# Activations as the stationary operand, four weight tiles per product: the second part of a one-core encoder block

## The chip, the cores and the metric

The kernel runs on one core of a Trainium2 chip. The metric is the time of one execution on the device, in microseconds (us). A separate profiled execution gives the trace and the page of the profile.

## What is computed

One encoder layer on 256 tokens of 2048 features, all in fp32:

```python
u = rmsnorm(h, g1);  z = u @ w_in          # [B_a C_a V_a | q k v | gate_a gate_b]
y_a = (b_a * dwconv3(c_a * v_a)) @ w_out_a
y_b = windowed_attention(rope(q), rope(k), v, sink) @ w_o_attn
h = h + (sigmoid(gl_a + ba) * y_a + sigmoid(gl_b + bb) * y_b) @ w_mix_out
up = dwconv3(rmsnorm(h, g2) @ ffn_w_up) + bias;  a, g = split(up)   # 2 x 5632
h = h + (silu(a) * g) @ ffn_w_down
return rmsnorm(h, g3)
```

Nearly all the work is in the matrix products. There are 243 MB of fp32 weights (60.8 million), each of which is used once, with 256 tokens.

## The kernel before

Features lie on the partitions (128 at a time, a *tile*), the 256 tokens in the free dimension. A job computes one tile of 128 output features: for each of its k blocks of 128 input features it takes one block of 128x128 weights and the activations of that block (128 features x 256 tokens). To keep fp32 accuracy in the fp32r format, both are split into a high and a low part, and three of the four cross products are summed: high weights with high activations, high weights with low activations, low weights with high activations. High and low activations lie side by side, so the first two are one product of 512 columns (line 215), and the third is one of 256 columns (line 216). The weights are the stationary operand and the activations move. One bank of PSUM holds both halves of the sum; `total` (L243) copies one half to SBUF on ScalarE (L245) and adds the other to it on VectorE (L249). A *pair* below is the two products of one k block of one tile.

`run` (L131) cuts all jobs into chunks of eight weight blocks (512 KB) and writes out the order of every engine by hand. For each chunk c it issues the fetch of chunk c+6 on SyncE's DMA queue (`fetch`, L155, five buffers), the high part of chunk c+3 on ScalarE (`high`, L165), the low part of chunk c+2 on VectorE (`low`, L180, three buffers), and then the products of chunk c. After each chunk one step of every open epilogue is issued; an epilogue is a generator, and `yield 1` means "go on after the next chunk". So the engines' queues hold fetches, splits and epilogues in a fixed order, and an instruction that waits holds up those issued after it on its engine. `turns` swaps the two products of a few pairs (`turned` in `run`), so that there a 256-column product follows a 256-column one, and a 512-column one a 512-column one.

The stages, in the order of the work: a first part (q, k, v, conv branch, attention); the gates (32 tiles of `w_in`, 16 k blocks each); `w_oa` and `w_o` in turn (16 tiles each, 8 k blocks); `w_mix` (16 tiles, 16 k blocks); `w_up` (88 tiles, 16 k blocks); `w_dn` (16 tiles, 44 k blocks). At the start of `w_mix`, `w_up` and `w_dn` a few jobs are interleaved by k (`outer_first`, L629), so that their first products don't wait for the last results of the stage before. The last tile of `w_dn` is computed in halves of the tokens, to shorten the tail (`finale`, L687). After the attention and after the second norm, `turns` is asked for.

The epilogues: `scaled` (L367) multiplies by the norm's factor; `epi_gate`, `epi_ya`, `epi_yb`, `epi_mix`, `epi_up` and `epi_dn` (L587 to L685) do the rest. `sumsq` (L288) sums squares for the next norm on GpSimd, two instructions for each tile.

Of the kernel before, what the change touches and what calls it, by code (L numbers as in the profile page):

```python
# [26 lines left out]
CH = 8  # L27
WIDE = 6
# [23 lines left out]
def hybrid_block_kernel(ctx: ExitStack, tc: tile.TileContext, head, wide, xT, w_in, w_oa, w_o, w_mix, w_up, w_dn, vec, cst, out):  # L52
# [4 lines left out]
    spool = ctx.enter_context(tc.tile_pool(name="spool", bufs=2))  # L57
    lin = ctx.enter_context(tc.tile_pool(name="lin", bufs=3, space=PSUM))
# [4 lines left out]
    ct = cpool.tile([P, C_END], F32, tag="ct", name="ct")  # L63
# [3 lines left out]
    ident = ct[:, C_ID : C_ID + P]  # L67
# [62 lines left out]

    def run(groups):  # L131

# [5 lines left out]
        for size, jobs, wide in groups:  # L138
            n = jobs[0][1]
            if wide:  # L140
                for k in range(n):
                    chunks.append((None, [(job, k) for job in jobs], wide))
                continue
            for k0 in range(0, n, size):
                k1 = min(n, k0 + size)
                for job in jobs:
                    chunks.append((job[0][:, k0:k1, :], [(job, k) for k in range(k0, k1)], None))
        raws, his, los, banks = {}, {}, {}, {}

        def pieces(c):  # L150

            n = len(chunks[c][1])
            return ((0, 2), (2, n)) if c < 3 else ((0, n),)

        def fetch(c):  # L155
            w, blocks, pre = chunks[c]
            if pre is not None:
                raws[c] = pre(0, c)
            else:
                raw = wpool.tile([P, CH, P], F32, tag="raw", name="raw", bufs=5)  # L160
                nc.sync.dma_start(raw[:, : len(blocks), :], w)
                raws[c] = lambda a, b, raw=raw: raw[:, a:b, :]


        def high(c):  # L165
            _, blocks, pre = chunks[c]
            if pre is not None:
                pre(1, c)
            (_, _, _, _, *halves), k0 = blocks[0]
            if halves:  # L170
                last = lazy("last", lambda: cpool.tile([P, FT, P], F32R, tag="B", name="last"))
                his[c] = last[:, k0 : k0 + len(blocks), :]
            else:
                his[c] = wpool.tile([P, CH, P], F32R, tag="whi", name="whi")
            for a, b in pieces(c):
                nc.scalar.copy(his[c][:, a:b, :], raws[c](a, b))  # L176
            if pre is not None:
                pre(2, c)
# [11 lines left out]
        for c, (_, blocks, _) in enumerate(chunks):  # L190
# [7 lines left out]
            for i, (job, k) in enumerate(blocks):  # L198
                _, n, rhs, epi, *halves = job
# [5 lines left out]
                a, last, half = rhs(k), k == n - 1, bool(halves and k)  # L205
                if order["due"] and n == KT:
# [7 lines left out]
                products = [  # L214
                    lambda: nc.tensor.matmul(both, hi[:, i, :], moving, start=k == 0, stop=last and turned),  # L215
                    lambda: nc.tensor.matmul(  # L216
                        ps[:, 0:T], lo[:, i, :], a[:, 0:T], start=False, stop=last and not turned
                    ),
                ]
# [23 lines left out]
    def total(ps, dst=None):  # L243
        b = spool.tile([P, T], F32, tag="evb", name="evb")
        nc.scalar.copy(b, ps[:, T : 2 * T])  # L245
        yield 1
        if dst is None:
            dst = spool.tile([P, T], F32, tag="evt", name="evt")
        nc.vector.tensor_tensor(dst, ps[:, 0:T], b, op=ALU.add)  # L249
        return dst  # L250

    rr = {}

    def inv_rms(parts, r, tag="tp"):
# [6 lines left out]
        r0 = spool.tile([P, T], F32, tag="sq", name="r0")[:, 0:n]  # L261
        nc.scalar.activation(r0, acc, AF.Ln, bias=eps)
        v = spool.tile([P, T], F32, tag="evt", name="nv")[:, 0:n]
# [4 lines left out]
        t = spool.tile([P, T], F32, tag="evs", name="nt")[:, 0:n]  # L268
# [19 lines left out]
    def sumsq(k, src, acc):  # L288
        sq = spool.tile([P, T], F32, tag="sq", name="sq") if k else acc
# [5 lines left out]
    p1 = p0.enter_context(tc.tile_pool(name="p1", bufs=1))  # L295


    HEAD = KT + 4 * P
    hd = p1.tile([P, HEAD], F32, tag="hd", name="hd")
    hb = p1.tile([P, WIDE, P], F32, tag="hb", name="hb")  # L300

# [53 lines left out]
    def r1():  # L355
# [5 lines left out]
        yield from inv_rms([sq1[:, 0, :]], new_r("r1"))  # L361
# [5 lines left out]
    def scaled(ps, dst=None):  # L367
        t = yield from total(ps)
        if dst is None:
            dst = spool.tile([P, T], F32, tag="evs", name="evs")  # L370
        nc.vector.tensor_tensor(dst, t, rr["r"], op=ALU.mult)
        return dst
# [228 lines left out]
    def epi_yb(m, ps):  # L601
        gates = box["gates"]
        t = yield from total(ps)
        nc.vector.tensor_tensor(t, t, gates[:, KT + m, :], op=ALU.mult)
# [6 lines left out]
    def epi_mix(m, ps):  # L611
        yield 1
        for i in range(2):
            nc.vector.tensor_tensor(x[:, m, :], x[:, m, :], ps[:, i * T : i * T + T], op=ALU.add)
# [8 lines left out]
    for i in range(2 * KT):  # L623
        groups.append(single(w_in[len(rest) + i], KT, xr, lambda ps, i=i: epi_gate(i, ps)))
    for m in range(KT):
        groups.append(single(w_oa[m], 8, lambda k: box["B"][:, k, :], lambda ps, m=m: epi_ya(m, ps)))
        groups.append(single(w_o[m], 8, lambda k: box["B"][:, 8 + k, :], lambda ps, m=m: epi_yb(m, ps)))

    def outer_first(jobs, n):  # L629

        groups.append((4, jobs[:n], None))
        groups.extend((CH, [job], None) for job in jobs[n:])

    outer_first([(w_mix[m], KT, lambda k: merged()[:, k, :], lambda ps, m=m: epi_mix(m, ps)) for m in range(KT)], 3)


    def start_ffn():
# [4 lines left out]
        return actA, actC  # L642
# [7 lines left out]
    def r2():  # L650
        nc.scalar.preload_act_table_set("natural_log_exp_and_others")
        yield from inv_rms([acc2], new_r("r2"))
        later(10, turns)

    def epi_up(i, which, ps):
        c = i + which * FT
        t = yield from scaled(ps)
        yield 1
        lazy("act", start_ffn)
# [10 lines left out]
        else:  # L670
            s = half.pop(i)
# [4 lines left out]
    def epi_dn(m, ps):  # L676
        yield 1
# [4 lines left out]
        for i in range(2):  # L682
            nc.vector.tensor_tensor(h, h, ps[:, i * T : i * T + T], op=ALU.add)
# [3 lines left out]
    def finale(ps):  # L687
# [24 lines left out]
        def norm(half):  # L712

            h = x[:, m, cols(half)]
            sq = spool.tile([P, T], F32, tag="sq", name="sq")[:, 0:H]
            nc.scalar.square(sq, h)
            nc.tensor.matmul(sums[half], ones, sq, start=False, stop=True)  # L717
            ln = spool.tile([P, T], F32, tag="evb", name="ln")[:, 0:H]
            nc.scalar.activation(ln, sums[half], AF.Ln, bias=eps)  # L719
            v = spool.tile([P, T], F32, tag="evt", name="nv")[:, 0:H]  # L720
            nc.vector.tensor_scalar(v, sums[half], EPS, None, op0=ALU.add)
            r0 = spool.tile([P, T], F32, tag="sq", name="r0")[:, 0:H]
            nc.scalar.activation(r0, ln, AF.Exp, scale=-0.5)
            nc.scalar.mul(h, h, col(V_GFIN + m))
            t = spool.tile([P, T], F32, tag="evs", name="nt")[:, 0:H]
# [40 lines left out]
    jobs = []  # L766
    for i in range(FT):
        for which in range(2):
            epi = lambda ps, i=i, which=which: epi_up(i, which, ps)
            jobs.append((w_up[2 * i + which], KT, lambda k: hsplit()[:, k, :], epi))  # L770
    outer_first(jobs, 3)
    jobs = [(w_dn[m], FT, act, lambda ps, m=m: epi_dn(m, ps)) for m in range(KT - 1)]
    outer_first(jobs + [(w_dn[KT - 1], FT, act, finale, True)], 2)
# [23 lines left out]
def _layout(a):  # L797
# [5 lines left out]

    def cols(v):
# [15 lines left out]
    order += range(g0, g0 + 2 * D)  # L820
    up = []
    for i in range(FT):
# [22 lines left out]
        "w_oa": tiles(a["w_out_a"][0]),  # L845
        "w_o": tiles(a["w_o_attn"][0][att, :]),
        "w_mix": tiles(a["w_mix_out"][0]),
        "w_up": tiles(a["ffn_w_up"][0][:, up]),
        "w_dn": tiles(a["ffn_w_down"][0]),
# [23 lines left out]
```

## Time and profile before

| | |
|---|---|
| time, 3 runs | 1331.04 us median (1330.96 to 1332.08) |
| profiled execution | 1332.0 us, of which the span of its instructions is 1330.2 us |
| TensorE (PE) busy | 1320.0 us, 99% of the span |
| VectorE (DVE) busy | 955.7 us, 72% |
| ScalarE (ACT) busy | 723.1 us, 54% |
| GpSimd (POOL) busy | 70.1 us, 5% |
| DMA | 255.54 MB, mean 192 GB/s, queue q1 59.1% of 16 engines |
| first and last start of a 512-column product: gates and all before | 6.3 to 409.1 us |
| `w_oa` and `w_o` | 409.4 to 497.8 us |
| `w_mix` | 498.2 to 586.6 us |
| `w_up` | 586.9 to 1075.2 us |
| `w_dn` | 1075.6 to 1304.0 us, then the last tile |

How to read it: a matmul's recorded duration runs from its start to the modelled end of its drain, so neighbours overlap and durations must not be added; the step from one start to the next is what a product costs. PE is matmuls and PEld weight loads, which run beside them. A group of instructions names the line, the engine, the operation, the tiles (out<-in), the shapes, the count, then busy time and mean duration. A wait of an engine is named by who ended it.

### The profile page before, as it was taken

The numbers are of one execution on the slowest core, as the hardware profiler recorded it, in microseconds if no ns is written. First come the engines' busy times: TensorE is split into PE (matmuls) and PEld (weight loads), VectorE is DVE, ScalarE is ACT, GpSimd is POOL, SyncE is SP. The second block draws the span as 40 slices with busy tenths as digits, with TensorE's granted clock in tenths as the row PEclk, the third lists the DMA queues.
The fourth block names the chain that finished last, engine by engine and source line by source line (L and its number), as shares of the span: only waits on it lengthen the run. The fifth ranks groups of instructions, "written<-read, shape, count | busy, mean of one in ns | idle before, by whom it ended". The sixth has DMA issues, their size and how long they took to land.

```text
span 1330.2 us, 20480 instructions
## 1 busy us (share of the span) xinstructions
PE 1320.0 (99%) x7686; PEld 1161.4 (87%) x7686; DVE 955.7 (72%) x1508; ACT 723.1 (54%) x1151; POOL 70.1 (5%) x66
## 2 busy tenths in 40 slices
PE   9999999999999999999999999999999999999997
PEld 8888888888888888888888888888888888888886
DVE  7888777555557887668888888888888865445444
ACT  7667665555555545446555555555555545444442
POOL 0000000000000002430000000000000001111211
PEclk9999999999999999999999999999999999999999
DMA  8786545555555547547555555555555557666663
GB/s 309 234 243 200 199 158 175 182 191 190 191 189 190 190 143 236 188 141 235 190 190 190 191 190 190 190 191 190 191 190 190 174 153 236 194 186 183 197 191 104
DMA packets 76676, 255.54 MB, mean 192 GB/s; under 512 B 8864, under 2 KB 9248, under 8 KB 76576
## 3 DMA queue, kind: packets, MB, share of 16 engines
q1 hardware_dynamic: 76144, 253.44, 59.1%
q8 instruction: 60, 0.98, 0.3%
q10 hardware_dynamic: 432, 0.79, 0.2%
q14 instruction: 40, 0.33, 0.1%
HBM read 248.16 MB, written 2.10 MB: 188 GB/s over the span
## 4 chain that ended last, share of the span: by engine, by line
PE 99%; DVE 0%; ACT 0%; POOLq 0%; issue 0%; DVEq 0%; ACTq 0%
PE ps L215 63%; PE ps L216 33%; PE av L491 1%; PE ptp L478 1%; PE warm L311 0%; PE s L448 0%; PE s L449 0%; PE more L695 0%; POOLq L868 0%; DVE y L737 0%; DVE r L729 0%; DVE x L702 0%; PE nps L259 0%; ACT ln L719 0%; PE nps L717 0%
## 5 line engine op out<-in xcount | busy, mean ns | idle before, releaser
L187 DVE TENSOR_TENSOR wlo<-raw,whi 128x1024 fp32r<-128x1024 f32 (+3 forms) x493 | 568.0, 1154 | 314.4 <-PE ps L216 222.2
L176 ACT CAST whi<-raw 128x1024 fp32r<-128x1024 f32 (+3 forms) x493 | 488.2, 992 | 326.4 <-PE ps L215 187.7
L215 PE MATMUL ps<-hs,whi 128*128 128x512 f32 x1408 | 488.2, 391 | 0.0
L216 PE MATMUL ps<-hs,wlo 128*128 128x256 f32 x1408 | 393.6, 280 | 0.0
L215 PE MATMUL ps<-xs,whi 128*128 128x512 f32 x1088 | 377.4, 392 | 0.0
L215 PEld LDWEIGHTS ps<-hs,whi 128*128 128x128 f32 x1408 | 263.0, 187 | 57.4
L216 PE MATMUL ps<-xs,wlo 128*128 128x256 f32 x1088 | 300.6, 280 | 0.0
L216 PEld LDWEIGHTS ps<-hs,wlo 128*128 128x128 f32 x1408 | 266.1, 189 | 0.4
L215 PEld LDWEIGHTS ps<-xs,whi 128*128 128x128 f32 x1088 | 202.2, 188 | 42.9 <-issue 0.4
L216 PEld LDWEIGHTS ps<-xs,wlo 128*128 128x128 f32 x1088 | 205.8, 189 | 2.4
L245 ACT COPY evb<-ps 128x256 f32<-128x256 f32 x188 | 70.0, 373 | 197.9 <-PE ps L216 194.2
L215 PE MATMUL ps<-actC,whi 128*128 128x512 f32 x420 | 146.2, 391 | 0.0
L216 PE MATMUL ps<-actC,wlo 128*128 128x256 f32 x448 | 124.4, 280 | 0.0
L215 PEld LDWEIGHTS ps<-actC,whi 128*128 128x128 f32 x420 | 78.5, 187 | 17.2
L215 PE MATMUL ps<-ya_att,whi 128*128 128x512 f32 x256 | 88.8, 391 | 0.0
L215 PE MATMUL ps<-ms,whi 128*128 128x512 f32 x256 | 88.8, 391 | 0.0
L216 PEld LDWEIGHTS ps<-actC,wlo 128*128 128x128 f32 x448 | 84.8, 189 | 0.0
L215 PE MATMUL ps<-actA,whi 128*128 128x512 f32 x240 | 83.8, 391 | 0.0
L249 DVE TENSOR_TENSOR evt<-ps,evb 128x256 f32<-128x256 f32 x178 | 74.4, 418 | 0.7 <-ACT evb L245 0.7
L216 PE MATMUL ps<-ya_att,wlo 128*128 128x256 f32 x256 | 71.7, 280 | 0.0
L216 PE MATMUL ps<-ms,wlo 128*128 128x256 f32 x256 | 71.7, 280 | 0.0
L216 PE MATMUL ps<-actA,wlo 128*128 128x256 f32 x256 | 70.9, 280 | 0.0
(144 smaller groups left out, 1050.3 us busy)
## 6 DMA issues: line engine op xcount, KB each, us to landing
raw<-in_w_up_dram SPq DMA_DIRECT2D x170, 512.0 KB, 4.1
raw<-in_w_in_dram SPq DMA_DIRECT2D x124, 512.0 KB, 3.6
raw<-in_w_dn_dram SPq DMA_DIRECT2D x70, 512.0 KB, 4.4
raw<-in_w_mix_dram SPq DMA_DIRECT2D x26, 512.0 KB, 4.3
raw<-in_w_dn_dram SPq DMA_DIRECT2D x36, 256.0 KB, 2.7
raw<-in_w_oa_dram SPq DMA_DIRECT2D x16, 512.0 KB, 3.2
raw<-in_w_o_dram SPq DMA_DIRECT2D x16, 512.0 KB, 3.2
raw<-in_wide_dram SPq DMA_DIRECT2D x14, 512.0 KB, 5.2
```

The lines of the kernel that those rows point to most:

```text
L176: nc.scalar.copy(his[c][:, a:b, :], raws[c](a, b))
L187: nc.vector.tensor_tensor(los[c][:, a:b, :], raw(a, b), his[c][:, a:b, :], op=ALU.subtract)
L215: lambda: nc.tensor.matmul(both, hi[:, i, :], moving, start=k == 0, stop=last and turned),
L216: lambda: nc.tensor.matmul(ps[:, 0:T], lo[:, i, :], a[:, 0:T], start=False, stop=last and not turned),
L245: nc.scalar.copy(b, ps[:, T : 2 * T])
L249: nc.vector.tensor_tensor(dst, ps[:, 0:T], b, op=ALU.add)
L478: nc.tensor.transpose(tp[:, b, n * P : (n + 1) * P], p[:, n, b * P : (b + 1) * P], ident)
L491: nc.tensor.matmul(o[64 * e : 64 * e + 64, 0:T], vtok[:, b, v0 : v0 + HD], pT[e][:, b, :], start=b == 0, stop=b == 1)
```

## The change

From the gates on, the roles of the operands are exchanged. A job is now a *quad*: four tiles, 512 output features. For each k block the activations stand (128 features x 128 tokens, four times: high and low part of the two halves of the tokens) and the weights of the four tiles move, 512 columns at a time. Each k block of a quad takes six products of 512 columns; the results have tokens on the partitions and features in the free dimension, in two banks. A chunk is two k blocks of a quad, still eight weight blocks and 512 KB, so `fetch`, `high` and `low` are as before.

The rest of the kernel wants features on the partitions. So VectorE reads each bank with a transpose of 32x32 blocks into `qd`, one DMA writes `qd` to a buffer in DRAM, and four DMAs read it back into `qf`, with the blocks in the right places. All five are issued on SyncE's queue, the writing one a step after the first transpose, the reading ones a step later; the four epilogues begin two steps after that, the first three a step apart. `total` is gone from them; they read `qf` from SBUF. At most two quads of the gates, `w_oa`, `w_o` and `w_mix` are under way at once, and one of `w_up` and `w_dn`; another waits. Three sets of two banks go round.

All of `w_oa` now comes before `w_o`. The first two quads of `w_mix` and of `w_up` are interleaved by k, `w_dn` not. The weights are laid out anew in DRAM (four tiles' columns side by side; 2 KB of one k block of a quad are contiguous on each partition). The last four tiles of `w_dn` stay as they were. `turns` is now asked for once after the quads, and not in them. Some buffers of SBUF move to other pools.

The diff, cut to its core:

```diff
+    def quad_banks():
+        q = taken[0] % 3
+        taken[0] += 1
+        where = [(aps, "s0"), (aps, "s1")], [(aps, "tp2"), (aps, "av")], [(lin, "ps"), (lin, "ps")]
+        return [pool.tile([P, QUAD * P], F32, tag=tag, name="pq") for pool, tag in where[q]]
...
+                if kind == ["quad"]:
+                    if k == 0:
+                        banks[id(job)] = quad_banks()
+                        was_quad[0] = True
+                    a, last = rhs(k), k == n - 1
+                    wh, wl = (
+                        w[:, QUAD * i : QUAD * i + QUAD, :].rearrange("p q f -> p (q f)") for w in (hi, lo)
+                    )
+                    for h, ps in enumerate(banks[id(job)]):
+                        ah, al = (a[:, o + h * P : o + h * P + P] for o in (0, T))
+                        nc.tensor.matmul(ps, ah, wh, start=k == 0, stop=False)
+                        nc.tensor.matmul(ps, al, wh, start=False, stop=False)
+                        nc.tensor.matmul(ps, ah, wl, start=False, stop=last)
+                    if last:
+                        ended.append(job)
+                    continue
+                if was_quad[0]:
+                    was_quad[0] = False
+                    turns()
...
+    def quad(*epis, stage, bufs):
+        def go(banks):
+            while under_way[0] >= bufs:
+                yield 1
+            under_way[0] += 1
+            pool = stage()
+            d = pool.tile([P, 4, 2, QUAD * S], F32, tag="qd", name="qd", bufs=bufs)
+            for h, ps in enumerate(banks):
+                if h:
+                    yield 1
+                nc.vector.transpose(d[:, :, h, :], ps)
+            f = pool.tile([P, 4, 2, QUAD, S], F32, tag="qf", name="qf", bufs=bufs)
+
+            way = turn.tile([4, S, 4, 2 * QUAD * S], F32, tag="way", name="way")
+            nc.sync.dma_start(way.rearrange("a j b x -> (a j) (b x)"), d.rearrange("p b h x -> p (b h x)"))
+            yield 1
+            for b in range(4):
+                nc.sync.dma_start(
+                    f[S * b : S * b + S].rearrange("p a h m i -> p a (h m i)"),
+                    way[:, :, b, :].rearrange("a j x -> j a x"),
+                )
+            for _ in range(2):
+                yield 1
+            for m, epi in enumerate(epis):
+                begin(epi, f[:, :, :, m, :].rearrange("p a h i -> p h a i"))
+                if m < 2:
+                    yield 1
+            under_way[0] -= 1
...
+    def scaled_quad(f):
+        dst = spool.tile([P, T], F32, tag="evs", name="evs", bufs=4)
+        nc.vector.tensor_tensor(by_block_of_tokens(dst), f, by_block_of_tokens(rr["r"]), op=ALU.mult)
         return dst
...
-    def epi_ya(m, ps):
-        t = yield from total(ps)
-        gates = box["gates"]
-        nc.vector.tensor_tensor(gates[:, m, :], gates[:, m, :], t, op=ALU.mult)
+    def epi_ya(m, f):
+        g = by_block_of_tokens(box["gates"][:, m, :])
+        nc.vector.tensor_tensor(g, g, f, op=ALU.mult)
...
+    quads(w_gate, KT, xr, epi_gate, stage1, range(2 * KT))
+    quads(w_oa, 8, lambda k: box["B"][:, k, :], epi_ya, stage1, range(KT))
+    quads(w_o, 8, lambda k: box["B"][:, 8 + k, :], epi_yb, stage1, range(KT))
+    quads(w_mix, KT, lambda k: merged()[:, k, :], epi_mix, stage1, range(KT), side=2)
...
+    quads(w_up, KT, lambda k: hsplit()[:, k, :], lambda t, f: epi_up(*t, f), stage2, up, side=2)
+    quads(w_dn, FT, act, epi_dn, stage2, range(KT - QUAD))
+    for m in range(KT - QUAD, KT - 1):
+        groups.append(single(w_end[m - KT + QUAD], FT, act, lambda ps, m=m: epi_dn(m, ps)))
+    groups.append((CH, [(w_end[QUAD - 1], FT, act, finale, "halves")], None))
```

More of the change, by code (lines that the diff above doesn't have):

```diff
@@ L27 @@
 CH = 8
+QUAD = 4
 WIDE = 6
@@ L51, in hybrid_block_kernel @@
 @with_exitstack
-def hybrid_block_kernel(ctx: ExitStack, tc: tile.TileContext, head, wide, xT, w_in, w_oa, w_o, w_mix, w_up, w_dn, vec, cst, out):
+def hybrid_block_kernel(
+    ctx: ExitStack, tc: tile.TileContext, head, wide, xT, w_in, w_gate, w_oa, w_o, w_mix, w_up, w_dn, w_end, vec, cst, out
+):
     nc = tc.nc
@@ L146, in run, with size @@
                 for job in jobs:
-                    chunks.append((job[0][:, k0:k1, :], [(job, k) for k in range(k0, k1)], None))
+                    w = job[0][:, k0:k1].rearrange("p k (q f) -> p (k q) f", f=P)
+                    chunks.append((w, [(job, k) for k in range(k0, k1)], None))
         raws, his, los, banks = {}, {}, {}, {}
+        was_quad = [False]
+        def size(c):
+            w, blocks, _ = chunks[c]
+            return len(blocks) if w is None else w.shape[1]
         def pieces(c):
-            n = len(chunks[c][1])
+            n = size(c)
             return ((0, 2), (2, n)) if c < 3 else ((0, n),)
@@ L160, in fetch @@
                 raw = wpool.tile([P, CH, P], F32, tag="raw", name="raw", bufs=5)
-                nc.sync.dma_start(raw[:, : len(blocks), :], w)
+                nc.sync.dma_start(raw[:, : w.shape[1], :], w)
                 raws[c] = lambda a, b, raw=raw: raw[:, a:b, :]
@@ L204, in run @@
                 ps = banks[id(job)]
-                a, last, half = rhs(k), k == n - 1, bool(halves and k)
-                if order["due"] and n == KT:
+                a, last, half = rhs(k), k == n - 1, bool(kind and k)
+                if order["due"] and n >= KT:
                     order["turned"] = {pairs[0] + d for d in order["due"]}
@@ L243, in total @@
     def total(ps, dst=None):
-        b = spool.tile([P, T], F32, tag="evb", name="evb")
+        b = ev.tile([P, T], F32, tag="evb", name="evb")
         nc.scalar.copy(b, ps[:, T : 2 * T])
@@ L247, in total, with by_block_of_tokens, inv_rms @@
         if dst is None:
-            dst = spool.tile([P, T], F32, tag="evt", name="evt")
+            dst = ev.tile([P, T], F32, tag="evt", name="evt")
         nc.vector.tensor_tensor(dst, ps[:, 0:T], b, op=ALU.add)
         return dst
+    S = 32
+    def by_block_of_tokens(a):
+        return a.rearrange("p (h a i) -> p h a i", h=2, a=4)
+    under_way = [0]
+    def quad(*epis, stage, bufs):
[25 more added lines that the diff above has]
+            under_way[0] -= 1
+        return go
     rr = {}
-    def inv_rms(parts, r, tag="tp"):
+    def inv_rms(parts, r, pool, tag="tp"):
         n = r.shape[-1]
@@ L260, in inv_rms @@
         yield 1
-        r0 = spool.tile([P, T], F32, tag="sq", name="r0")[:, 0:n]
+        r0 = spool.tile([P, T], F32, tag="sq", name="r0", bufs=1)[:, 0:n]
         nc.scalar.activation(r0, acc, AF.Ln, bias=eps)
-        v = spool.tile([P, T], F32, tag="evt", name="nv")[:, 0:n]
+        v = pool.tile([P, T], F32, tag="evt", name="nv")[:, 0:n]
         nc.vector.tensor_scalar(v, acc, EPS, None, op0=ALU.add)
@@ L266, in inv_rms @@
         yield 1
-        t = spool.tile([P, T], F32, tag="evs", name="nt")[:, 0:n]
+        t = spool.tile([P, T], F32, tag="evs", name="nt", bufs=4)[:, 0:n]
         nc.vector.tensor_tensor(t, r0, r0, op=ALU.mult)
@@ L288, in sumsq @@
     def sumsq(k, src, acc):
-        sq = spool.tile([P, T], F32, tag="sq", name="sq") if k else acc
+        sq = spool.tile([P, T], F32, tag="sq", name="sq", bufs=1) if k else acc
         nc.gpsimd.tensor_tensor(sq, src, src, op=ALU.mult)
@@ L360, in r1 @@
         yield 1
-        yield from inv_rms([sq1[:, 0, :]], new_r("r1"))
+        yield from inv_rms([sq1[:, 0, :]], new_r("r1"), ev)
         for name, c in (("cos", C_COS), ("sin", C_SIN)):
@@ L369, in scaled @@
         if dst is None:
-            dst = spool.tile([P, T], F32, tag="evs", name="evs")
+            dst = spool.tile([P, T], F32, tag="evs", name="evs", bufs=4)
         nc.vector.tensor_tensor(dst, t, rr["r"], op=ALU.mult)
+        return dst
+    def scaled_quad(f):
+        dst = spool.tile([P, T], F32, tag="evs", name="evs", bufs=4)
+        nc.vector.tensor_tensor(by_block_of_tokens(dst), f, by_block_of_tokens(rr["r"]), op=ALU.mult)
         return dst
@@ L609, in hybrid_block_kernel, with epi_mix @@
     acc2 = spool.tile([P, T], F32, tag="acc", name="acc2", bufs=1)
[L611 to L614, printed above, removed]
+    def epi_mix(m, f):
+        xm = by_block_of_tokens(x[:, m, :])
+        nc.vector.tensor_tensor(xm, xm, f, op=ALU.add)
         yield 1
@@ L621, in epi_mix, with quads @@
         gsplit_lo(hsplit()[:, m, :], x[:, m, :], col(V_GFFN + m))
[L623 to L634, printed above, removed]
+    def quads(w, n, rhs, epi, stage, tiles, side=1):
+        jobs = []
+        for q in range(len(tiles) // QUAD):
+            four = [lambda f, t=t: epi(t, f) for t in tiles[QUAD * q : QUAD * q + QUAD]]
+            jobs.append((w[q], n, rhs, quad(*four, stage=stage, bufs=2 if stage is stage1 else 1), "quad"))
+        groups.append((2, jobs[:side], None))
+        groups.extend((2, [job], None) for job in jobs[side:])
+    quads(w_gate, KT, xr, epi_gate, stage1, range(2 * KT))
+    quads(w_oa, 8, lambda k: box["B"][:, k, :], epi_ya, stage1, range(KT))
+    quads(w_o, 8, lambda k: box["B"][:, 8 + k, :], epi_yb, stage1, range(KT))
+    quads(w_mix, KT, lambda k: merged()[:, k, :], epi_mix, stage1, range(KT), side=2)
     def start_ffn():
@@ L641, in start_ffn @@
         actC = box["p2"].tile([P, FT - KT, 2 * T], F32R, tag="actC", name="actC")
-        return actA, actC
+        box["act"] = actA, actC
+        return box["p2"]
+    stage2 = lambda: lazy("ffn", start_ffn)
     def act(k):
@@ L651, in r2, with epi_up @@
         nc.scalar.preload_act_table_set("natural_log_exp_and_others")
-        yield from inv_rms([acc2], new_r("r2"))
-        later(10, turns)
-    def epi_up(i, which, ps):
+        yield from inv_rms([acc2], new_r("r2"), stage1())
+    def epi_up(i, which, f):
         c = i + which * FT
-        t = yield from scaled(ps)
+        t = scaled_quad(f)
         yield 1
-        lazy("act", start_ffn)
         p2 = box["p2"]
@@ L670, in epi_up @@
         else:
+            while i not in half:
+                yield 1
+            yield 1
             s = half.pop(i)
@@ L681, in epi_dn @@
         h = x[:, m, :]
-        for i in range(2):
-            nc.vector.tensor_tensor(h, h, ps[:, i * T : i * T + T], op=ALU.add)
+        if m < KT - QUAD:
+            h4 = by_block_of_tokens(h)
+            nc.vector.tensor_tensor(h4, h4, ps, op=ALU.add)
+        else:
+            for i in range(2):
+                nc.vector.tensor_tensor(h, h, ps[:, i * T : i * T + T], op=ALU.add)
         sumsq(m, h, box["acc3"])
@@ L764, in finale @@
         scale(1, 12, 16, nc.gpsimd, nc.sync)
[L766 to L773, printed above, removed]
+    up = [(i, which) for i in range(FT) for which in range(2)]
+    quads(w_up, KT, lambda k: hsplit()[:, k, :], lambda t, f: epi_up(*t, f), stage2, up, side=2)
[3 more added lines that the diff above has]
+    groups.append((CH, [(w_end[QUAD - 1], FT, act, finale, "halves")], None))
     run(groups)
@@ L802, in tiles, with quads @@
         return np.ascontiguousarray(w.reshape(k // P, P, n // P, P).transpose(2, 1, 0, 3))
+    def quads(w):
+        k, n = w.shape
+        w = w.reshape(k // P, P, n // (QUAD * P), QUAD, 4, P // 4).transpose(2, 1, 0, 4, 3, 5)
+        return np.ascontiguousarray(w).reshape(n // (QUAD * P), P, k // P, QUAD * P)
     def cols(v):
@@ L844, in _layout @@
         "w_in": tiles(w[:, order]),
[L845 to L849, printed above, removed]
+        "w_gate": quads(w[:, g0 : g0 + 2 * D]),
+        "w_oa": quads(a["w_out_a"][0]),
+        "w_o": quads(a["w_o_attn"][0][att, :]),
+        "w_mix": quads(a["w_mix_out"][0]),
+        "w_up": quads(a["ffn_w_up"][0][:, up]),
+        "w_dn": quads(a["ffn_w_down"][0][:, : D - QUAD * P]),
+        "w_end": tiles(a["ffn_w_down"][0][:, D - QUAD * P :]),
         "vec": np.ascontiguousarray(vec),
```

44 lines of the change are left out of this document (23 added, 21 removed).

## The prediction

> **What bounds the kernel now.** First the page: busy shares, the clock line and the chain of work that ended last.
>
> ```profile
> PE 1320.0 (99%) x7686; PEld 1161.4 (87%) x7686; DVE 955.7 (72%) x1508; ACT 723.1 (54%) x1151; POOL 70.1 (5%) x66
> ...
> PEclk9999999999999999999999999999999999999999
> ...
> PE 99%; DVE 0%; ACT 0%; POOLq 0%; issue 0%; DVEq 0%; ACTq 0%
> PE ps L215 63%; PE ps L216 33%; PE av L491 1%; PE ptp L478 1%; PE warm L311 0%; PE s L448 0%; PE s L449 0%; PE more L695 0%; POOLq L868 0%; DVE y L737 0%; DVE r L729 0%; DVE x L702 0%; PE nps L259 0%; ACT ln L719 0%; PE nps L717 0%
> ```
>
> TensorE runs without a gap, and 96% of the chain is the two products. So what a product costs decides, as long as nothing starves TensorE. The durations in the groups overlap; I take steps from start to start. First the windows view of a long stretch of `w_up` beside two others (columns: length, then busy time and count of PE, PEld, DVE, ACT, POOL, clock, DMA share, GB/s), then the timeline of PE at three places: the steady alternation, the last tile, where all products have 256 columns, and a turned pair, where two of 512 columns follow each other ("x2").
>
> ```profile
> 10.00:40.00 30.00, 30.00 (x174) 26.31 (x173) 23.98 (x33) 22.87 (x43) 0.00 (x0) 1.00 0.84 293
> 420.00:490.00 70.00, 70.00 (x405) 61.72 (x405) 58.93 (x102) 36.72 (x62) 0.00 (x0) 1.00 0.54 179
> 640.00:1070.00 430.00, 430.00 (x2482) 379.13 (x2481) 352.54 (x582) 246.64 (x388) 0.00 (x0) 1.00 0.58 187
> ```
> ```profile
> 700.12 0.39 PE L215 MATMUL ps<-hs,whi 128*128 128x512 f32 x1
> 700.35 0.28 PE L216 MATMUL ps<-hs,wlo 128*128 128x256 f32 x1
> 700.47 0.39 PE L215 MATMUL ps<-hs,whi 128*128 128x512 f32 x1
> ```
> ```profile
> 1308.41 0.28 PE L215 MATMUL ps<-actC,last 128*128 128x256 f32 x1
> ...
> 1309.13 0.28 PE L215 MATMUL ps<-actC,last 128*128 128x256 f32 x1
> ```
> ```profile
> 619.73 0.63 PE L215 MATMUL ps<-hs,whi 128*128 128x512 f32 x2
> 620.20 0.28 PE L216 MATMUL ps<-hs,wlo 128*128 128x256 f32 x1
> ```
>
> The reader is to see four numbers. A pair costs 430.00 us / 1241 = 346.5 ns. Within it the step after the 512 columns is 0.23 us, after the 256 columns 0.12. Where only 256-column products follow each other, the six from 1308.41 to 1309.13 cost 120 ns each. And two neighbouring 512-column products cost 0.47 us / 2 = 235 ns each.
>
> **The change, part by part: the products.** Columns streamed stay the same: a k block of a quad has 6 x 512 = 3072, four pairs have 4 x 768 = 3072. Weight loads fall from eight to six. So the gain is two loads' share, if a load has a share. If a product costs c for each column and L for its load, then 256c + L = 120 and 768c + 2L = 346.5, so c = 0.416 ns and L = 13.5 ns: 512 columns cost 226.5 ns by themselves. By the step in the alternation it would be 230, by the neighbours in the turned pair 235. I take 226.5, since it comes from two steady stretches (the last tile's products, and 2482 of `w_up`), where a start's own jitter cancels; the 235 stands in a place where the order is disturbed on purpose, and keeps its place as the other end. A k block of a quad then costs 6 x 226.5 = 1359 ns against 4 x 346.5 = 1386: 27 ns less.
>
> The k blocks: gates 8 quads x 16, `w_oa` and `w_o` 4 x 8 each, `w_mix` 4 x 16, `w_up` 22 x 16, `w_dn` 3 x 44, in sum 740. That gives 740 x 27 ns = 20.0 us less. With 230 ns it is 740 x 6 = 4.4 us less, with 235 ns 740 x 24 = 17.8 us more. It comes out even at 1386 / 6 = 231.0 ns.
>
> The first part, the last four tiles of `w_dn` and the tail stay. The dropped turned pairs (two sets of four) are worth some 10 ns each: nothing.
>
> **Splits and epilogues.** A chunk has twelve products, 12 x 226.5 = 2.72 us, against 8 x 346.5 = 2.77. The groups that move or bound what is new:
>
> ```profile
> L187 DVE TENSOR_TENSOR wlo<-raw,whi 128x1024 fp32r<-128x1024 f32 x417 | 512.5, 1230 | 262.7 <-PE ps L216 180.5 <-issue 76.0 <-ACT whi L176 3.1
> L176 ACT CAST whi<-raw 128x1024 fp32r<-128x1024 f32 x417 | 438.7, 1053 | 277.3 <-PE ps L215 159.2 <-issue 112.0 <-DMA raw<-in_w_mix_dram 1.9
> L249 DVE TENSOR_TENSOR evt<-ps,evb 128x256 f32<-128x256 f32 x178 | 74.4, 418 | 0.7 <-ACT evb L245 0.7
> L245 ACT COPY evb<-ps 128x256 f32<-128x256 f32 x188 | 70.0, 373 | 197.9 <-PE ps L216 194.2 <-DVE evt L249 3.2
> L371 DVE TENSOR_TENSOR evs<-evt,r 128x256 f32<-128x256 f32 x120 | 51.0, 425 | 4.1
> L457 DVE TENSOR_REDUCE st<-s 128x2 f32<-128x512 f32 x16 | 11.1, 691 | 0.6
> L292 POOL TENSOR_TENSOR acc<-acc,sq 128x256 f32<-128x256 f32 x29 | 42.5, 1465 | 2.3
> L290 POOL TENSOR_TENSOR sq<-x 128x256 f32<-128x256 f32 x29 | 22.8, 785 | 209.0 <-DVE x L683 166.4 <-DVE x L614 42.5
> ```
>
> A quad loses four copies on ACT (4 x 373 ns) and four adds on DVE (4 x 418 = 1.67 us); the multiplication (425 ns) stays, reading runs of 32. It gains two transposes of 128x512 from PSUM. No row shows one; the nearest is the reduction of 128x512 from PSUM, 0.69 us; at twice that a quad has 1.1 us more DVE work, at that price 0.3 us less, and I take the row. All of it lies beside the 21.8 us of a quad's eight chunks (10.9 us in `w_oa` and `w_o`), where DVE was busy 82% (352.54 of 430.00) and 84% (58.93 of 70.00). GpSimd gets four tiles at once, 4 x (0.785 + 1.465) = 9.0 us; the second norm's product is issued ten chunks after the quad, the last tile comes three tiles of 44 pairs after it (46 us). Cost of all this: nothing.
>
> **The trip through DRAM.** It adds 0.5 MB out and 0.5 MB back for each of 45 quads, and five issues to SP's queue, where the weight fetches stand behind them. The rows:
>
> ```profile
> raw<-in_w_mix_dram SPq DMA_DIRECT2D x26, 512.0 KB, 4.3
> ...
> rot<-qkraw SPq DMA_DIRECT2D x20, 64.0 KB, 3.6
> ```
> ```profile
> L161 SPq DMA_DIRECT2D raw<-in_w_up_dram x182: 327/328/328, 569.2 to 1054.9; - x182
> ```
> ```profile
> L386 SPq DMA_DIRECT2D rot<-qkraw x20: 543/582/615, 44.2 to 93.6; - x20
> ```
> ```profile
> 480.26 19.21 SPq L161 DMA_DIRECT2D raw<-in_w_mix_dram  x8
> ```
> ```profile
> 490.31 0.62 ACT L176 CAST whi<-raw 128x512 fp32r<-128x512 f32 x1
> ```
> ```profile
> L215 PE MATMUL ps<-ms,whi x256: 391/391/391, 498.2 to 586.6; 128*128 128x512 f32 x128
> ```
>
> Bandwidth: a chunk needs 524 kB in 2.72 us, 193 GB/s; the trip adds 48 GB/s in eight-chunk quads and 96 in `w_oa` and `w_o`, at most 289 there. The stretch from 10 to 40 us moved 293 GB/s with PE busy 30.00 of 30.00 us. So bandwidth alone stops nothing.
>
> Waits: let t be the end of a quad's last product. DVE transposes (0.69), splits a chunk that waits for t as well (1.23), transposes again: the write is issued at t + 2.6, and lands by the 4.3 us of a 512 KB load at t + 7.2. SP stands there, then issues four reads of 128 KB on 32 partitions (the issue of `rot`, 0.58 each): t + 9.3 when it is free for the fetch that should have gone at t + 4. The fetch is 5 us late. In the rows the first `w_mix` fetch goes at 480.26 and ACT splits it at 490.31: less 4.3 for landing, 5.7 us of slack, and TensorE comes another 8 us later (its first product is at 498.2). Covered. The last read lands, by `rot`'s 3.6, at t + 12.6. DVE reaches the first epilogue after its split at t + 9.4 and waits there, with the split of the seventh chunk after the quad queued behind it; that split must be done at t + 6 x 2.72 = t + 16.3, so the reads may land until t + 15. Margin 2.4 us, no cost.
>
> Between stages: the last `w_o` quad's tiles are ready about eight chunks after its end (trip four, the epilogue's steps four), and `w_mix`, two quads interleaved, needs its k blocks 12 to 15 from its thirteenth chunk on. The same holds for `w_mix` to `w_up`; `w_dn` needs the last two `w_up` blocks in its 22nd chunk. Covered.
>
> **The sum.** 1332.0 us of the profiled execution less 20.0 is 1312.0. The runs' median is 1.0 us lower than that execution, so I forecast 1311 us.
>
> **The rivals.** (1) *The alternation's step*: a 512-column product costs 230 ns wherever it stands, the load's share being in the larger product. For it: the two steps of the timeline. Against it: 120 ns in the last tile, which 346.5 - 230 does not give. 1331.0 - 4.4 = 1326.6. (2) *Slower*: neighbouring 512-column products cost 235 ns, because loads then come at the wrong moment. Place: each of the 4440 products. Price 17.8 us; it decides from 231.0 ns on. For it: the only neighbours in the trace cost that. Against: they stand singly. 1348.8. (3) *The load vanishes* behind 512 columns: 512 x 0.416 = 213.0 ns, 108 ns less a k block, 79.9 us less in all: 1251. Against it: a 512-column product behind another of 512 columns cost 235, no less than elsewhere. [...] The steps of 230 and 235 ns here speak against it. (4) *The trip starves TensorE*: reads that land later than t + 15 stop it once for each quad; each microsecond over costs up to 45 us. Against: the 2.4 us of margin. For: with all 16 engines in use in `w_oa`, and writing to DRAM and reading back at once, no row shows the landing. Half a microsecond over beside the forecast's gain gives 1311 + 22 = 1333, a whole one 1356.
>
> **How the numbers follow.** Forecast 0.34, rival 1 0.24, rival 2 0.20, rival 3 0.08, rival 4 0.14. The range takes in the forecast with some 7 us below it, rivals 1 and 2, and rival 4 up to one microsecond: 1304 to 1356, leaving out rival 3 and half of rival 4, 0.15. A change of 0.2% (2.7 us) is about what a measurement of this kernel can tell. Faster: forecast, rival 3 and most of rival 1 (0.17), in sum 0.59. Same: the rest of rival 1 and a little of rival 4, 0.09. Slower: rivals 2 and 4, 0.32. The forecast's own range is 1304 to 1318.
>
> **What would show it.** [...] The transposes at 0.7 us; SP's waits for the write near 4 us; landing of reads near 3.6 us. Idle time of PE before `wlo` or `whi`, once a quad, would show rival 4. Wrong would be: a product below 222 or above 231 ns, or TensorE idle by more than 5 us between 232 us and the last tile.

## The result and the profile after

The changed kernel takes 1321.01 us (median of 4 runs, 1319.17 to 1322.85) against 1331.2 us (4 runs): a ratio of 0.9922, 95% interval 0.9905 to 0.9939. So it is faster by 10.2 us, where 20.0 were forecast. The profiled execution took 1320.97 us, its span is 1319.2 us, 11.0 less than before.

The page after: busy shares, then the chain of work that ended last, then the new transpose and, from the DMA part, the trip.

```profile
PE 1304.1 (99%) x6206; PEld 1090.2 (83%) x6206; DVE 941.7 (71%) x1390; ACT 678.9 (51%) x971; POOL 62.5 (5%) x66
...
PE 94%; DMA 3%; DVE 2%; issue 1%; SPq 0%; ACT 0%; POOLq 0%; DVEq 0%; ACTq 0%
PE pq L231 24%; PE pq L230 24%; PE pq L229 24%; PE ps L253 13%; PE ps L254 7%; DMA qf<-way 1%; DMA way<-qd 1%; DVE wlo L206 1%; PE av L578 1%; PE ptp L565 1%; SPq L317 0%; PE warm L393 0%; DVE qd L310 0%; PE s L536 0%; PE s L535 0%
...
L310 DVE STREAM_TRANSPOSE qd<-pq 128x512 f32<-128x512 f32 x90 | 63.8, 709 | 9.6 <-PE pq L231 9.5
...
way<-qd SPq DMA_DIRECT2D x45, 512.0 KB, 2.9
qf<-way SPq DMA_DIRECT2D x180, 128.0 KB, 2.9
```

The chain had been TensorE alone, 99%. Now 3% are DMA, the trip out (`way<-qd`) and back (`qf<-way`), and 2% DVE. So the trip has come onto the path somewhere. TensorE's steady step first, in the timeline of `w_up`; L229 and L230 are the products of the high weights, L231 of the low ones.

```profile
700.15 0.39 PE L229 MATMUL pq<-whi,hs 128*128 128x512 f32 x1
700.38 0.39 PE L230 MATMUL pq<-whi,hs 128*128 128x512 f32 x1
700.61 0.39 PE L231 MATMUL pq<-wlo,hs 128*128 128x512 f32 x1
700.83 0.39 PE L229 MATMUL pq<-whi,hs 128*128 128x512 f32 x1
```

Three products in 0.68 us: 227 ns each. Over the whole trace nearly all steps are 227 or 226 ns, two of the one to one of the other, which is 226.67 where nothing waits. That is the forecast's 226.5. The windows view finds the place of the loss (length, then busy time and count of PE, PEld, DVE, ACT, POOL, clock, DMA share, GB/s):

```profile
250.00:400.00 150.00, 150.00 (x664) 124.20 (x663) 86.60 (x97) 69.89 (x82) 0.00 (x0) 1.00 0.75 242
640.00:1050.00 410.00, 410.00 (x1811) 339.49 (x1810) 339.31 (x547) 226.71 (x311) 0.00 (x0) 1.00 0.74 243
1100.00:1240.00 140.00, 140.00 (x619) 115.95 (x618) 70.85 (x64) 58.87 (x61) 14.65 (x15) 1.00 0.68 208
```
```profile
470.00:515.00 45.00, 42.60 (x182) 33.43 (x181) 34.26 (x61) 19.89 (x29) 0.00 (x0) 1.00 0.78 260
545.00:570.00 25.00, 22.46 (x91) 17.82 (x90) 18.64 (x23) 10.86 (x16) 13.20 (x15) 0.93 0.62 203
```

In the gates, `w_up` and `w_dn` PE is busy all the time. It loses 2.4 us at the end of `w_o` and the start of `w_mix`, and 2.5 us behind the two interleaved quads of `w_mix` (they end at 540.64), where the clock column is also below 1. An idle engine is not the whole loss: the products behind a stall were slow too (steps of 0.33 and 0.43 us behind the one at 563.54 below). So I add up, over all starts of a quad's products, the step to the next start less 226.67 ns: 0.2 us in the gates, 1.65 in `w_oa` and `w_o`, 7.0 in `w_mix`, 0.2 in `w_up`, nothing in `w_dn`. In sum 9.1 us, of which 4.0 stand between 470 and 515 us and 4.7 between 545 and 571. 20.0 - 9.1 = 10.9, and the span shrank by 11.0. So the account closes, as far as such an account can: what stands before and behind the quads differs by some 1 us each between the profiled executions of the kernels here. The products gave what was forecast, and stalls in two places took back nearly half.

The second place, in the timeline of PE (in brackets the idle time before, and what ended it):

```profile
563.54 0.39 PE L230 MATMUL pq<-whi,ms 128*128 128x512 f32 x1
565.85 0.50 PE L231 MATMUL pq<-wlo,ms 128*128 128x512 f32 x1 [1.92 <-DVE wlo L206]
566.18 0.52 PE L229 MATMUL pq<-whi,ms 128*128 128x512 f32 x1
566.50 0.63 PE L230 MATMUL pq<-whi,ms 128*128 128x512 f32 x1
566.93 0.63 PE L231 MATMUL pq<-wlo,ms 128*128 128x512 f32 x1
```

TensorE waits 1.92 us for the low weights (`wlo`), and from 566.50 on the steps are 0.43 us, nearly double, for some 3 us. What VectorE did before:

```profile
554.48 0.43 DVE L699 TENSOR_TENSOR x<-x,qf 128x256 f32<-128x256 f32 x1 [3.86 <-DMA qf<-way]
554.82 1.22 DVE L206 TENSOR_TENSOR wlo<-raw,whi 128x1024 fp32r<-128x1024 f32 x1
555.96 2.47 DVE L699 TENSOR_TENSOR x<-x,qf 128x256 f32<-128x256 f32 x3
...
559.23 1.63 DVE L206 TENSOR_TENSOR wlo<-raw,whi 128x1024 fp32r<-128x1024 f32 x1
...
564.04 1.75 DVE L206 TENSOR_TENSOR wlo<-raw,whi 128x1024 fp32r<-128x1024 f32 x1
```

Two things at once. VectorE stood 3.86 us for the trip's reads, with the next split behind that wait. And then its instructions were slow: an addition took 0.82 us where 0.43 is usual, a split 1.63 to 1.75 where it is 1.23. GpSimd was at its sums of squares then (`POOL` 13.20 us of those 25).

### The profile page after: what moved, and what is told of

Its sections match the earlier page's. It is cut to its first block, busy times and chain, and to the rows that moved or that the text cites. A ratio compares the mean times of both kernels' runs of the same rounds, so it can differ in the third digit from the quotient of the medians.

```text
span 1319.2 us, 17559 instructions
## 1 busy us (share of the span) xinstructions
PE 1304.1 (99%) x6206; PEld 1090.2 (83%) x6206; DVE 941.7 (71%) x1390; ACT 678.9 (51%) x971; POOL 62.5 (5%) x66
## 4 chain that ended last, share of the span: by engine, by line
PE 94%; DMA 3%; DVE 2%; issue 1%; SPq 0%; ACT 0%; POOLq 0%; DVEq 0%; ACTq 0%
PE pq L231 24%; PE pq L230 24%; PE pq L229 24%; PE ps L253 13%; PE ps L254 7%; DMA qf<-way 1%; DMA way<-qd 1%; DVE wlo L206 1%; PE av L578 1%; PE ptp L565 1%; SPq L317 0%; PE warm L393 0%; DVE qd L310 0%; PE s L536 0%; PE s L535 0%
## 5 line engine op out<-in xcount | busy, mean ns | idle before, releaser
L229 PE MATMUL pq<-whi,hs 128*128 128x512 f32 x704 | 274.0, 389 | 0.0
L231 PE MATMUL pq<-wlo,hs 128*128 128x512 f32 x704 | 273.9, 389 | 0.0
L230 PE MATMUL pq<-whi,hs 128*128 128x512 f32 x704 | 273.9, 389 | 0.0
L253 PE MATMUL ps<-xs,whi 128*128 128x512 f32 x576 | 200.3, 394 | 0.0
L254 PE MATMUL ps<-xs,wlo 128*128 128x256 f32 x576 | 158.0, 280 | 0.0
L229 PEld LDWEIGHTS pq<-whi,hs 128*128 128x128 f32 x704 | 132.1, 188 | 27.6
L230 PEld LDWEIGHTS pq<-whi,hs 128*128 128x128 f32 x704 | 132.1, 188 | 27.4
L231 PEld LDWEIGHTS pq<-wlo,hs 128*128 128x128 f32 x704 | 132.1, 188 | 27.3
L254 PEld LDWEIGHTS ps<-xs,wlo 128*128 128x128 f32 x576 | 108.9, 189 | 1.9
L229 PE MATMUL pq<-whi,xs 128*128 128x512 f32 x256 | 99.7, 390 | 0.0
L230 PE MATMUL pq<-whi,xs 128*128 128x512 f32 x256 | 99.6, 389 | 0.0
L231 PE MATMUL pq<-wlo,xs 128*128 128x512 f32 x256 | 99.6, 389 | 0.0
L458 DVE TENSOR_TENSOR evs<-qf,r 128x256 f32<-128x256 f32 x120 | 48.0, 421 | 41.8 <-DMA qf<-way 41.7
L229 PE MATMUL pq<-whi,actC 128*128 128x512 f32 x168 | 65.4, 389 | 0.0
L230 PE MATMUL pq<-whi,actC 128*128 128x512 f32 x168 | 65.4, 389 | 0.0
L231 PE MATMUL pq<-wlo,actC 128*128 128x512 f32 x168 | 65.4, 389 | 0.0
L229 PEld LDWEIGHTS pq<-whi,xs 128*128 128x128 f32 x256 | 48.0, 188 | 10.4 <-issue 0.4
L230 PEld LDWEIGHTS pq<-whi,xs 128*128 128x128 f32 x256 | 48.0, 188 | 10.0
```

Source lines behind the costliest of these rows:

```text
L229: nc.tensor.matmul(ps, ah, wh, start=k == 0, stop=False)
L230: nc.tensor.matmul(ps, al, wh, start=False, stop=False)
L231: nc.tensor.matmul(ps, ah, wl, start=False, stop=last)
L254: lambda: nc.tensor.matmul(ps[:, 0:T], lo[:, i, :], a[:, 0:T], start=False, stop=last and not turned),
L458: nc.vector.tensor_tensor(by_block_of_tokens(dst), f, by_block_of_tokens(rr["r"]), op=ALU.mult)
```

## Experiments

Theory A: GpSimd holds up VectorE. Theory B: the trip's reads come later than the step at which the epilogue wants them. Both name places of the same stall, so each is taken away by itself. A third run takes the trip away altogether, a fourth tests what a product costs, and three more follow from what these show.

**No sums on GpSimd.** All but the first tile's sum of squares in `w_mix` is left out, so the second norm is of one tile.

```diff
-        sumsq(m, x[:, m, :], acc2)
+        if m == 0:
+            sumsq(m, x[:, m, :], acc2)
```

> Leaves out 15 of the 16 sums of squares of the w_mix epilogues on GpSimd (the second norm is then of one tile only). Theory A (GpSimd reading SBUF holds up VectorE's instructions with two SBUF operands, so the splits of the weights come late): the x additions of the w_mix epilogues fall from a median of 0.83 to 0.42 us, the splits there from up to 1.76 to 1.23 us, the TensorE stalls at 560 to 566 us and the half-clock stretch behind them (5.3 us in all over the 226.7 ns of a product) go, time 1315 to 1317 us. Theory B (late reads of the trip and late fetches alone): the stalls at 560 to 566 us stay over 3 us, time 1320 to 1322.

1316.75 us, ratio 0.9886 (0.9871 to 0.9901). The additions at L699 in the source view (durations min/median/max), first of the changed kernel, then of this run:

```profile
L699 DVE TENSOR_TENSOR x<-x,qf x16: 418/830/960, 547.5 to 606.4; 128x256 f32<-128x256 f32 x16
```
```profile
L699 DVE TENSOR_TENSOR x<-x,qf x16: 416/419/426, 548.2 to 600.2; 128x256 f32<-128x256 f32 x16
```

The additions are back at 0.42 us. The stall at 560 us and the half clock behind it, 4.7 us by the steps and not the 5.3 I wrote, are gone: there is no step over 300 ns between 515 and 610 us. The sum over 226.67 ns in `w_mix` falls from 7.0 to 2.9 us. What is left there, and 1.9 us in `w_o`, stands between 487 and 515 us, where theory B has its place: three waits of 1.0 to 1.8 us. So GpSimd's sums are needed for the second stall, and they aren't all.

**Epilogues a chunk later.** The whole computation; one more step between the reads and the first epilogue.

```diff
-            for _ in range(2):
+            for _ in range(3):
                 yield 1
             for m, epi in enumerate(epis):
```

> The four epilogues of each quad begin one chunk later after the reads are issued (three steps in place of two). Theory B (VectorE and ScalarE stand waiting for the trip's reads with the next splits queued behind): VectorE's waits for qf (41.7 us before the multiplications and 29 before the additions and products) fall below a third, the four stalls at 477 to 514 us go (3.2 us), time 1317 to 1319. Theory A: those waits cost nothing at the end of w_mix, so the 5.3 us at 560 to 570 us stay. If both: the first go, the second stay.

1314.48 us, ratio 0.9873 (0.9858 to 0.9887): its interval lies wholly below that of the changed kernel. The waits of VectorE for the reads in the changed kernel, then here:

```profile
DVE evs L458 <- DMA qf<-way: 41.7, 28, 3.9
```
```profile
DVE evs L458 <- DMA qf<-way: 4.5, 9, 0.9
```
```profile
470.00:515.00 45.00, 45.00 (x200) 37.29 (x199) 40.03 (x69) 22.29 (x33) 0.00 (x0) 1.00 0.84 282
545.00:570.00 25.00, 23.84 (x104) 19.07 (x103) 22.89 (x27) 12.15 (x17) 13.22 (x15) 1.00 0.61 200
```

Between 470 and 515 us PE is busy all of 45.00 us, 200 products where there had been 182. At 561 to 565 us two stalls remain, 1.8 us over 226.67 ns in sum, and the clock stays at 1.00. It gave more than I expected (6.5 us, not 2 to 4): the late reads had a share in the second stall as well, since VectorE comes into that stretch 3.9 us late.

**No trip.** The epilogues read the transposed blocks where VectorE put them, so features and tokens are not in their places.

```diff
-            f = pool.tile([P, 4, 2, QUAD, S], F32, tag="qf", name="qf", bufs=bufs)
...
+            f = d.rearrange("p b h (m i) -> p b h m i", i=S)
             yield 1
```

> Leaves out the DMA to DRAM and back: the epilogues read the transposed blocks from where VectorE put them, so the features and tokens are not in their places; everything else is issued as before, at the same steps. If the trip (waits of VectorE for reads, of SyncE for the write, the DMA traffic) makes all of the loss: no stall over 0.3 us in any quad, sum over 226.7 ns under 0.6 us, time 1311 to 1313. If GpSimd makes the greater part: 3 to 5 us stay at the end of w_mix, time 1315 to 1317.

1313.12 us, ratio 0.9860 (0.9844 to 0.9877). Two waits are left, steps of 0.52 and 0.54 us at 558 and 561 us, 0.9 us in `w_mix` in all. The sum over all quads is 1.3 us, where I had written under 0.6 for the trip alone. So the trip made the greater part of the loss, 7.8 of 9.1 us, and GpSimd alone, with VectorE on time, less than one. The two are not additive: of the kernel's time 4.3 us go without GpSimd's sums, 7.9 without the trip.

**Twice the loads.** The whole computation; from a quad's second k block on each product is made as two of 256 columns with the same stationary block.

```diff
-                        nc.tensor.matmul(ps, ah, wh, start=k == 0, stop=False)
...
+                        step_ = 2 * P if k else QUAD * P
+                        for c0 in range(0, QUAD * P, step_):
+                            c1 = c0 + step_
+                            nc.tensor.matmul(ps[:, c0:c1], ah, wh[:, c0:c1], start=k == 0, stop=False)
...
```

> From the second k block of a quad on, each product of 512 columns is made as two of 256 with the same stationary block: twice the weight loads, the same columns, 695 k blocks. [...] Rival D (the load is hidden whatever the length, and a quad's products cost 226.7 for another reason): below 114 ns, no more than 5 us.

1376.02 us (one run). In its timeline:

```profile
800.06 0.28 PE L233 MATMUL pq<-whi,hs 128*128 128x256 f32 x1
800.18 0.28 PE L234 MATMUL pq<-wlo,hs 128*128 128x256 f32 x1
800.30 0.28 PE L232 MATMUL pq<-whi,hs 128*128 128x256 f32 x1
800.42 0.28 PE L233 MATMUL pq<-whi,hs 128*128 128x256 f32 x1
```

120 ns each, as in the last tile of the kernel before, and 226.67 for 512 columns: 106.7 ns for 256 columns, and 13.3 ns for each product at both lengths. 695 x 6 products more at 13.3 ns are 56 us; on top of the changed kernel's 1321.01 that gives 1377 us, 1 us from what was measured. In the kernel before and in the changed one each product has a load of its own (6206 of both in the page after), so whether the 13.3 ns are the load or another fixed cost of a product isn't shown. At 117 ns, the short step of the alternation, it would be 31 us more, 1352; that falls, and so does rival D, below 114 ns.

**Sums spread in time.** With the later epilogues, the sums of squares were to be given to GpSimd one tile a chunk.

```diff
...
-        sumsq(m, x[:, m, :], acc2)
+        slot[0] = max(slot[0] + 1, now[0])
+        at(slot[0], lambda: sumsq(m, x[:, m, :], acc2))
...
```

> The whole computation, with the epilogues one chunk later as in the run before and with the sixteen sums of squares of w_mix given to GpSimd at most one tile a chunk, the second norm three chunks after the last. Theory A+B (late reads at the start of w_mix, GpSimd against VectorE at its end): the 1.8 us of TensorE stalls left at 561 to 565 us go, sum over 226.7 ns in all quads under 0.8 us, time 1312 to 1313.5. Rival (what is left there comes from the late weight fetches behind the trip on SyncE's queue): the stalls stay, 1314 to 1315.

1314.61 us, ratio 0.9871 (0.9857 to 0.9886), and the stalls are those of the later epilogues, 1.8 us. That isn't the rival's doing, though its number came out. GpSimd in the timeline of this run:

```profile
557.88 0.68 POOL L369 TENSOR_TENSOR sq<-x 128x256 f32<-128x256 f32 x1
558.64 0.80 POOL L371 TENSOR_TENSOR acc<-acc,sq 128x256 f32<-128x256 f32 x1
559.52 0.68 POOL L369 TENSOR_TENSOR sq<-x 128x256 f32<-128x256 f32 x1
```

Nothing was spread: the tiles follow each other as before. Issuing them later in the hand-written order could only have put them behind other work of GpSimd. Between 545 and 565 us it had no other: it starts 0.08 us after its last instruction, as above, or when `x` is there (at 549.54, after 2.17 us idle that the addition at L701 ended). The run tests nothing, and my edit was at fault.

**Squares on ScalarE.** With the later epilogues, ScalarE squares and GpSimd only adds. The whole computation.

```diff
...
-        sumsq(m, x[:, m, :], acc2)
+        sq = spool.tile([P, T], F32, tag="sq", name="sq", bufs=1) if m else acc2
+        nc.scalar.square(sq, x[:, m, :])
+        if m:
+            nc.gpsimd.tensor_tensor(acc2, acc2, sq, op=ALU.add)
```

> The whole computation, the epilogues one chunk later; the squares of the w_mix epilogues go to ScalarE, GpSimd keeps only the additions, unspread. By theory A half of GpSimd's reads remain: stalls of 0.5 to 1.2 us at the end of w_mix, 1313 to 1314.5; were ScalarE's order the limit, its casts come late and the stalls grow over 2 us.

1313.66 us (1312.49 to 1313.81), ratio 0.9861 (0.9845 to 0.9878). The windows view:

```profile
470.00:515.00 45.00, 45.00 (x200) 37.25 (x199) 40.69 (x69) 21.99 (x33) 0.00 (x0) 1.00 0.86 290
545.00:570.00 25.00, 25.00 (x112) 20.63 (x111) 20.21 (x27) 14.98 (x25) 6.57 (x7) 1.00 0.68 225
```

112 products where there had been 91, no stall in either place; in all quads 0.4 us over 226.67 ns. GpSimd's time in the stretch is halved. That is better than I expected: what GpSimd still reads costs TensorE nothing. This kernel is 7 us faster than the changed one, with the trip in it: what the trip had cost was its lateness, not its traffic. Against the later epilogues alone the intervals overlap, so there the gain is shown by the stalls of the trace and not by the time.

**The trip on GpSimd's queue.** The changed kernel with its five DMAs issued from GpSimd, so that no weight fetch stands behind them.

```diff
-            nc.sync.dma_start(way.rearrange("a j b x -> (a j) (b x)"), d.rearrange("p b h x -> p (b h x)"))
+            nc.gpsimd.dma_start(way.rearrange("a j b x -> (a j) (b x)"), d.rearrange("p b h x -> p (b h x)"))
...
-                nc.sync.dma_start(
+                nc.gpsimd.dma_start(
```

> The changed kernel with the trip's five DMAs issued from GpSimd's queue in place of SyncE's, so that no weight fetch stands behind them; the epilogues' steps as they were. If SyncE's hold makes the stalls (fetches late): no stall in w_o and the first half of w_mix, 1314 to 1317. If the reads themselves come too late for the epilogue's step: the waits of VectorE for qf stay or grow, stalls as before or longer, 1320 to 1330.

1480.73 us (one run). The trip's transfers there:

```profile
way<-qd POOLq DMA_DIRECT2D x45, 512.0 KB, 6.0
qf<-way POOLq DMA_DIRECT2D x180, 128.0 KB, 4.4
```

6.0 us from issue to landing in place of 2.9, and 4.4 in place of 2.9; the longest wait of the epilogues is 9.2 us, and stalls come in every stage from the gates on. The direction is what lateness of the reads would give, the size far more than I wrote. As the trip was slower on this queue, the run doesn't tell how much SyncE's hold by itself did; since the kernel with the squares on ScalarE has the trip on SyncE's queue and no stall, that hold costs nothing there.

## Why the prediction was right, and where not

**The product.** Right, and by its working: 226.5 ns solved from two steady stretches, 226.7 measured, 13.5 ns a product besides its columns against 13.3. Rivals 1 (230) and 2 (235) fall; the steps of 230 and 117 ns in the alternation were a shift of the starts between a long and a short product; their sum alone, 347, was a cost, and 226.7 + 120 is that sum. The 235 of the turned pairs does not come back in a steady run: in the changed kernel steps of 231 to 236 ns stand only in the first dozen products behind a stall or a change of work (the first quad at 232 us, the second norm's product at 616). Rival 3 falls too: it had 213.0 ns for a product of 512 columns, and this trace has 226.7, with a load for each.

**The transposes.** 0.709 us measured against 0.69 taken. Bandwidth came out too: 242 GB/s in eight-chunk quads against 241 forecast.

**The step that failed** is the one on waits, "Margin 2.4 us, no cost". From issue to landing the median was even shorter than I took (write 2.9 us for 4.3, reads 2.9 for 3.6). What I had overlooked is what stands before and behind the wait. I let the transposes begin at t, the end of a quad's products, and I counted only the split of the seventh chunk behind the wait. In `w_o`, where a quad has four chunks, the next quad ends just when the first epilogue begins, and its transposes stand behind that wait too. Here is a quad whose products end at t = 471.37, when the next quad's first product starts (L690 and L273 are lines of epilogues):

```profile
471.37 0.39 PE L229 MATMUL pq<-whi,ya_att 128*128 128x512 f32 x1
```
```profile
474.67 0.42 DVE L690 TENSOR_TENSOR gates<-gates,qf 128x256 f32<-128x256 f32 x1 [4.33 <-DMA qf<-way]
...
475.48 0.71 DVE L310 STREAM_TRANSPOSE qd<-pq 128x512 f32<-128x512 f32 x1
...
486.30 0.43 DVE L690 TENSOR_TENSOR gates<-gates,qf 128x256 f32<-128x256 f32 x1 [1.95 <-DMA qf<-way]
...
487.10 0.76 DVE L273 TENSOR_TENSOR ms<-gates,ms 128x256 fp32r<-128x256 f32 x2
487.77 0.71 DVE L310 STREAM_TRANSPOSE qd<-pq 128x512 f32<-128x512 f32 x1
488.41 1.18 DVE L206 TENSOR_TENSOR wlo<-raw,whi 128x1024 fp32r<-128x1024 f32 x1
```
```profile
489.65 0.50 PE L231 MATMUL pq<-wlo,ya_att 128*128 128x512 f32 x1 [0.99 <-DVE wlo L206]
```

Its first transpose comes at t + 4.1, behind the wait for the quad before it. Its last read lands at t + 14.9, which is still inside my t + 15, and yet TensorE waits: between the landing and the split stand epilogues and the transpose of the next quad, 2.1 us of work that I had left out. So the margin was 0.3 us and not 2.4, and the late transposes used up more than that. And the trip feeds on itself: late reads, late transposes, a late write, later reads. The chain of work that ended last (above in shares, here in order of time) has the writes of three rounds:

```profile
466.32 2.90 DMA way<-qd
...
478.74 2.91 DMA way<-qd
...
491.04 2.90 DMA way<-qd
```

From write to write it takes 12.4 and 12.3 us, where four chunks of TensorE are 10.9. Counted from the end of each quad, the eight writes of `w_oa` and `w_o` are issued after 2.7, 2.8, 3.4, 4.0, 5.8, 7.4, 8.5 and 8.8 us; I had 2.6 for all. At the second place two interleaved quads end together, at 540.64, which I had not looked at: SyncE issues the second quad's write at 544.80, behind the first one's reads, though its transposes were done at 542.7, and its last read lands at t + 13.7.

All this is rival 4, in its place and kind, but not "once for each quad" and 45 us: in the stages with eight chunks VectorE waits as well (41.7 us in all before the multiplications) and catches up. Its chance of 0.14 was too low; the forecast's product and this rival were both true. (A slip besides: four issues of 0.58 us from t + 7.2 on end at t + 9.5, not 9.3. Nothing hangs on it.)

**GpSimd** I had costed at nothing, as its 9.0 us a quad lie beside other work. They do, but VectorE's additions, and many of its splits, took longer there. Before, the addition read PSUM and SBUF, and 32 of them took 406 to 422 ns. Two of these ran beside GpSimd, at 518.67 us, and were no slower; a split, which reads both operands from SBUF, took 1.41 us beside it in place of 1.23 (nine of them, from 534 to 580 us; four others beside it, from 516 to 530, kept 1.22):

```profile
L614 DVE TENSOR_TENSOR x<-x,ps x32: 406/418/422, 513.4 to 588.6; 128x256 f32<-128x256 f32 x32
```
```profile
518.55 0.80 POOL L292 TENSOR_TENSOR acc<-acc,sq 128x256 f32<-128x256 f32 x1
...
518.67 0.86 DVE L614 TENSOR_TENSOR x<-x,ps 128x256 f32<-128x256 f32 x2
...
551.12 1.41 DVE L187 TENSOR_TENSOR wlo<-raw,whi 128x1024 fp32r<-128x1024 f32 x1 [0.37 <-PE ps L216]
```

Now the addition reads two operands from SBUF, and four tiles come at once, so that GpSimd's sums stand in a row beside additions and splits. The rows, on few cases: an addition took 0.41 and 0.42 us from PSUM beside GpSimd, 0.83 to 0.96 us from SBUF beside it (eleven additions), 0.42 from SBUF without it. Without GpSimd's sums the median fell from 0.83 to 0.42 us; by what they slow VectorE, no run shows. I had looked at the engine's busy time only, and not at what changed its operands and how many tiles come together; how much each of these two did, no run here tells apart.

The forecast of 1311 us would have been 2.7 us below the best kernel here that computes everything. The range (1304 to 1356) held the result, but the forecast's own range (1304 to 1318) did not: 1321 lies in the room that was kept for the rivals. Neither sign of being wrong showed, the second by a hair and because it counts idle time alone: from 232 us on TensorE was idle for 4.93 us, where 5 was the limit, and lost 9.1.

```profile
232.00:1295.00 1063.00, 1058.07 (x4719) 876.03 (x4720) 746.19 (x1031) 518.54 (x651) 57.51 (x58) 1.00 0.73 235
```

## What to carry to other kernels

A cost per product can be solved from two steady stretches with a different mix of lengths (226.5 ns here, 226.7 measured); single steps between unlike neighbours shifted it from one to the other (230 and 117 ns, where 226.7 and 120 were the costs). When a wait is added, list everything behind it on its engine up to the next round of the same loop, and compare the round with the shortest period there, not with the mean. When an operand moves from PSUM to SBUF, look who else reads SBUF at that time: the addition here went from 0.42 us to a median of 0.83.

## What was not expected of the hardware

After the longest of its stalls the changed kernel's TensorE clock was halved. The windows view:

```profile
566.20:569.50 3.30, 3.30 (x10) 2.53 (x9) 3.30 (x6) 0.00 (x0) 0.85 (x2) 0.51 0.52 159
```

The granted clock is 0.51, and the step from product to product was 427 ns; this cost 1.6 us. A product's step of 2.30 us stood before it, with one of 1.01 us 3.6 us earlier. Two shorter stalls had no such stretch behind them: steps of 1.38 and 1.63 us at 488 and 501 us of the same trace (clock 1.00 from 470 to 515 us). With the trip on GpSimd's queue, where TensorE waited 45 times for the low weights, up to 5.5 us, the mean clock of the run was 0.967. Whether the length of a stall alone decides, these runs don't show. At half clock the step was 427 ns, twice the 213.3 that 512 columns take at 106.7 ns for 256: the 13.3 ns of a product don't show there.
